# A hybrid encoder block on one core: projection pairs issued in traced order, merges and residual by accumulating transfers

## The chip, the core and the metric

The kernel runs on one core of a Trainium2 chip. The core has five engines, each with its own instruction queue: TensorE (PE in the profile, with its weight loads shown as PEld), VectorE (DVE), ScalarE (ACT), GpSimd (POOL) and SyncE (SP). Sixteen DMA engines move data between device memory and the on-chip memory; a transfer is asked for on the queue of SP, ACT or POOL. The metric is the device time of one execution in microseconds, the median of several runs.

## What is computed

One layer of an encoder on 1024 tokens of 1024 channels: a mixer with two branches, then an MLP. Cut from the reference:

```python
h = rmsnorm(x, g_pre_mix)
proj = jnp.einsum('bsd,de->bse', h, w_in)            # u_pool 512 wide | q | k | v, 8 heads of 64
y_pool = jnp.einsum('bsc,cd->bsd', multiscale_pool(u_pool, w_pool_mix, pool_scale), w_br_pool)
o_sb = stick_breaking_attention(q, k, v)
y_sb = jnp.einsum('bsc,cd->bsd', o_sb, w_br_sb)
gates = jax.nn.sigmoid(jnp.einsum('bsd,de->bse', h, w_gate) + b_gate)
merged = gates[..., :D_MODEL] * y_pool + gates[..., D_MODEL:] * y_sb
x = x + rmsnorm(jnp.einsum('bsd,de->bse', merged, w_out), g_post_mix)
h2 = rmsnorm(x, g_pre_mlp)
a = jnp.square(jax.nn.relu(jnp.einsum('bsd,df->bsf', h2, w_up)))
x = x + rmsnorm(jnp.einsum('bsf,fd->bsd', a, w_down), g_post_mlp)
```

Pooling takes, for each of four groups of 128 channels, the trailing mean over 2, 4, 8 or 16 tokens minus the token itself, then a 128 x 128 map. Stick-breaking attention weighs token s for token t by sigmoid(z_ts) times the product of (1 - sigmoid(z_tj)) over the tokens j between them.

## The kernel before

All tensors lie with channels on the 128 partitions and tokens along the free axis, in two halves h of 512 tokens. Every product runs in three passes: each operand is split into a high part (a cast on ACT) and a low part (source minus high part, on DVE), and PE adds high x high, high x low and low x high. One 128 x 128 weight block against 512 tokens is thus three matmuls (`mm3`, lines 96 to 106).

The Tile framework orders the instructions of each engine before the program runs: it takes the traced order as priority, simulates the engines, and lets whatever is ready go first. An edge (`issue_after`, `add_manual_dep`) keeps two instructions in a wanted order. The order that results is fixed; at run time an engine waits at the head of its queue.

The stages, in order of time:

- **Input** (`phase_in`). Norm of x, the u and v projections, and the operands of the pairs: b11, b21, b22 and the sums t1 to t4, each with a high and a low part (`fill_operand`, line 1056). Its end also traces the first pair's weights (lines 454 to 480): a1, the adds of lines 513 to 517, and the splits s0 (sb) and w (sa).
- **Projection pairs** (`phase_project`). Gates, q and k are done two output blocks at a time by Winograd's form of Strassen's scheme: seven products of half size in place of eight. The 12 pairs are listed in `PAIRS` (line 491): gates 0 to 4, then q and k, then gates 5 to 7. Each `product` (line 659) is 12 matmuls into one of seven PSUM banks that are taken in turn. Its order is a1 on b11, a1 on b21, sb on t2, sa on t3, sa on t1, a22 on t4, sb on b22. DVE and ACT evict the banks; `result` (line 527) puts a sigmoid on a gate and stores it to `gscr`, or splits q and k and stores them to `qscr`. The last pair but one begins the first two products of the last.
- **Beside the pairs.** After each product two generators advance one step: `sw_weights` (line 493), which loads and splits the next pair's weights through three raw buffers and four steps, and `later` (line 546), which does the pooling (window sums on DVE, four buffers m0 to m3, a split into ph and pq, two times three matmuls, stores to `yscr`) and then the values (`vpair`, `vs`, stores to `sscr`). In the first 36 products every sixth gives `later` a second step. Every third of the first 48 products lets POOL start one of 40 transfers that sum weights for the MLP in device memory (`weight_sums`, line 1285).
- **Attention** (`phase_attention`, line 947). For each half g and head: scores, sigmoid (ACT), a scan (DVE, line 791), transposes on PE (line 804), a split of them into ahi (ACT) and alo (DVE, line 815), and the product with v (line 830). Jobs fill PE in between, dealt by the list `deal` in line 959: `job_pool`, `job_merge` (line 900, gate times product, plus the pooled branch from `bscr`, then a split into mg) and `job_out`. `fetch` (line 731) loads their gates; tiles named gt have four buffers.
- **After attention** (`phase_post`, `chain`, line 1062). The second half's merges and output, then for each half h: norm, residual, second norm and the operands of the up product, issued in small steps (`yield` with a step number) beside the matmuls. The residual of h = 1 comes through xr tiles that SP loads.
- **MLP** (`phase_mlp`, `down`). First 32 half-products whose results go to `pscr`, then 16 up pairs of five products each. `pair_raw` (line 1152) loads a pair's weights, `pair_b` and `pair_a` add and split them, `quarter` (line 1229) loads two stored products on ACT's queue. Then the down product, with its own loads chained by `load_in` (line 1325), and the last norm.

Names of the profile: sw and dbr and d are PSUM banks, wraw and wrawx raw weights, whi and wlo a split in the common buffers, s0, s1, a0, a1 the splits of sb and a22, h and ht operands of the pairs, T a score tile.

## Time and profile before

| | us |
|---|---|
| median of 3 runs | 1281.68 |
| lowest, highest | 1280.98, 1282.2 |
| profiled execution | 1283.02 |
| its span, first to last instruction | 1281.1 |
| mean granted TensorE clock | 0.997 of full speed |

| transfers by queue | packets | MB | share of 16 engines |
|---|---|---|---|
| SP (q1) | 65696 | 165.28 | 37.2% |
| POOL (q0) | 30992 | 91.13 | 25.4% |
| ACT (q10) | 13536 | 25.57 | 6.1% |

How to read the rows below. A line such as L104 is the line of the kernel that issued the instruction; products all run through lines 102 to 106, so the tile names tell them apart. `[2.59 <-DVE u L699]` behind an instruction means that its engine was idle for 2.59 us before it, until the DVE instruction of line 699 that wrote u had ended. A row of stages gives, for each engine, busy time and instructions. Matmul durations overlap: each is shown from its start to its modelled end, while the next one has already begun. Instructions in a group row are counted behind an x, followed by their busy time and the mean of one in nanoseconds.

### The profile page before, as it was taken

The numbers are of one execution on the slowest core, as the hardware profiler recorded it, in microseconds if no ns is written. First come the engines' busy times: TensorE is split into PE (matmuls) and PEld (weight loads), VectorE is DVE, ScalarE is ACT, GpSimd is POOL, SyncE is SP. The second block draws the span as 40 slices with busy tenths as digits, with TensorE's granted clock in tenths as the row PEclk, the third lists the DMA queues.
The fourth block names the chain that finished last, engine by engine and source line by source line (L and its number), as shares of the span: only waits on it lengthen the run. The fifth ranks groups of instructions, "written<-read, shape, count | busy, mean of one in ns | idle before, by whom it ended". The sixth has DMA issues, their size and how long they took to land.

```text
span 1281.1 us, 16198 instructions
## 1 busy us (share of the span) xinstructions
PE 1247.4 (97%) x5707; PEld 1022.0 (80%) x5707; DVE 970.6 (76%) x1311; ACT 621.9 (49%) x994; POOL 179.3 (14%) x319
## 2 busy tenths in 40 slices
PE   9999989999989999999999999999999999999998
PEld 6887768887877877777778878888888888888887
DVE  8759687776588898777777978888865564776985
ACT  7247344333455556554556635545554443344452
POOL 1212112342101011101101002221221110001000
PEclk9999999999999999999999989999999999999999
DMA  6586878977898774346638756766549997556552
GB/s 217 167 228 173 247 185 252 327 244 240 324 314 315 236 222 137 80 109 220 216 123 286 216 203 224 252 218 242 198 164 318 302 305 241 197 197 246 185 202 67
DMA packets 110306, 283.00 MB, mean 221 GB/s; under 512 B 12465, under 2 KB 17585, under 8 KB 109073
## 3 DMA queue, kind: packets, MB, share of 16 engines
q1 hardware_dynamic: 65696, 165.28, 37.2%
q0 software_dynamic: 30992, 91.13, 25.4%
q10 hardware_dynamic: 13536, 25.57, 6.1%
q8 instruction: 45, 0.74, 0.2%
q14 instruction: 37, 0.29, 0.1%
HBM read 208.52 MB, written 94.37 MB: 236 GB/s over the span
## 4 chain that ended last, share of the span: by engine, by line
PE 59%; DVE 8%; DMA 3%; issue 2%; ACT 2%; ACTq 0%; DVEq 0%; SPq 0%
PE d L104 16%; PE d L106 16%; PE d L105 16%; PE o L830 2%; DVE T L791 2%; PE dbr L106 2%; PE dbr L105 2%; PE dbr L102 2%; PE at L804 2%; DMA wraw<-w 1%; DVE wlo L75 1%; DVE alo L815 1%; DMA gt<-gscr 1%; PE z L787 1%; PE z L784 1%
## 5 line engine op out<-in xcount | busy, mean ns | idle before, releaser
L105 PE MATMUL d<-blo,whi 128*128 128x512 f32 (+1 forms) x456 | 172.3, 378 | 0.0
L106 PE MATMUL d<-bhi,wlo 128*128 128x512 f32 (+1 forms) x456 | 171.9, 378 | 0.0
L104 PE MATMUL d<-bhi,whi 128*128 128x512 f32 (+1 forms) x456 | 168.7, 378 | 0.0
L105 PEld LDWEIGHTS d<-blo,whi 128*128 128x128 f32 x456 | 85.7, 188 | 16.1
L106 PEld LDWEIGHTS d<-bhi,wlo 128*128 128x128 f32 x456 | 85.8, 188 | 15.8
L104 PEld LDWEIGHTS d<-bhi,whi 128*128 128x128 f32 x456 | 85.5, 188 | 16.0
L791 DVE TENSOR_TENSOR_SCAN T<-T,past 128x256 f32<-128x256 f32 (+5 forms) x64 | 84.5, 1347 | 5.8 <-ACT T L789 5.5
L105 PE MATMUL d<-b_lo,whi 128*128 128x512 f32 x196 | 76.3, 390 | 0.5 <-DVE b_lo L1060 0.5
L104 PE MATMUL d<-b_hi,whi 128*128 128x512 f32 x196 | 75.3, 391 | 0.6 <-ACT b_hi L1059 0.6
L106 PE MATMUL d<-b_hi,wlo 128*128 128x512 f32 x196 | 74.8, 390 | 0.0
L75 DVE TENSOR_TENSOR wlo<-wraw,whi 128x1024 fp32r<-128x1024 f32 x45 | 54.9, 1219 | 24.4 <-ACT whi L74 24.4
L74 ACT CAST whi<-wraw 128x1024 fp32r<-128x1024 f32 x45 | 47.4, 1054 | 49.6 <-DMA wraw<-w 17.1
L814 ACT CAST ahi<-at 128x512 fp32r<-128x512 f32 (+1 forms) x96 | 44.6, 483 | 48.5 <-PE at L804 40.2
L815 DVE TENSOR_TENSOR alo<-at,ahi 128x512 fp32r<-128x512 f32 (+1 forms) x96 | 50.7, 549 | 19.8 <-ACT ahi L814 19.5
L1351 DVE TENSOR_TENSOR wlo<-slots_hi,whi 128x1024 fp32r<-128x1024 f32 x29 | 35.5, 1224 | 37.7 <-ACT whi L1349 37.6
L1349 ACT CAST whi<-slots_hi 128x1024 fp32r<-128x1024 f32 x29 | 30.5, 1052 | 68.5 <-PE d L105 62.3
L1349 ACT CAST whi<-slots_lo 128x1024 fp32r<-128x1024 f32 x27 | 28.4, 1054 | 63.4 <-PE d L105 53.1
L104 PE MATMUL sw<-h_hi,whi 128*128 128x512 f32 x144 | 56.5, 393 | 2.0 <-ACT vs L619 0.8
L105 PE MATMUL sw<-h_lo,whi 128*128 128x512 f32 x144 | 56.1, 389 | 0.0
L106 PE MATMUL sw<-h_hi,wlo 128*128 128x512 f32 x144 | 55.5, 390 | 0.1
L104 PE MATMUL d<-t_hi,whi 128*128 128x512 f32 x132 | 52.7, 399 | 2.5 <-ACT whi L1166 2.5
L789 ACT ACTIVATE T<-z 128x256 f32<-128x256 f32 (+3 forms) x96 | 44.3, 500 | 19.9 <-PE z L787 10.9
(443 smaller groups left out, 3425.7 us busy)
## 6 DMA issues: line engine op xcount, KB each, us to landing
wraw<-w SPq DMA_DIRECT2D x57, 512.0 KB, 4.9
ext_b<-ascr SPq DMA_DIRECT2D x40, 512.0 KB, 7.1
wscr<-w POOLq DMA_DIRECT2D x32, 512.0 KB, 8.9
slots_hi<-w SPq DMA_DIRECT2D x10, 1024.0 KB, 7.7
slots_lo<-w SPq DMA_DIRECT2D x10, 1024.0 KB, 8.4
qq<-qscr SPq DMA_DIRECT2D x32, 256.0 KB, 5.9
pscr<-p SPq DMA_DIRECT2D x32, 256.0 KB, 4.5
u<-pscr ACTq DMA_DIRECT2D x32, 256.0 KB, 4.6
```

Source lines behind the costliest of these rows:

```text
L74: nc.scalar.copy(hi, raw)
L75: self.last_lo = nc.vector.tensor_sub(lo, raw, hi.bitcast(F32)).ins
L102: nc.tensor.matmul(ps, wh, rh, start=first and i == 0, stop=False)
L104: nc.tensor.matmul(ps, wh, rh, start=first and i == 0, stop=False)
L105: nc.tensor.matmul(ps, wh, rl, start=False, stop=False)
L106: self.last_mm = nc.tensor.matmul(ps, wl, rh, start=False, stop=last and i == n - 1).ins
L789: self.after = nc.scalar.activation(f, z[:, :n], AF.Sigmoid, scale=-1.0)
L791: nc.vector.tensor_tensor_scan(f[:, ::-1], f[:, ::-1], past[:, ::-1], 1.0, ALU.mult, ALU.max)
L814: nc.scalar.copy(hi[:, c:], at[:, c:])
L815: nc.vector.tensor_sub(lo[:, c:], at[:, c:], hi[:, c:].bitcast(F32))
L1349: last_split[0] = nc.scalar.copy(hi, src).ins
L1351: last_split[1] = nc.vector.tensor_sub(lo, src, hi.bitcast(F32)).ins
```

## The change

- **Order.** `in_order` adds an edge from each instruction to the next one of the same engine, for everything that is traced in the loop over the pairs on PE, DVE, ACT and POOL. SP is left out. The input stage, with the first pair's weights, is traced before the loop.
- **Weights.** A split is now two steps, high part and low part (`split_steps`), and every product gives two steps to the weights, with the step of `later` between them. A pair's loads are asked for in the first step of the pair before; six empty steps (three products) stand ahead of its first split. A generator that has steps left goes on in the next pair. In the input stage each call is doubled.
- **Pooling and values.** `later` gets one step a product. Window buffers alternate, ph and pq are split by halves of 512 tokens through one buffer, each half's three matmuls come one step after its split, the next u is loaded before the mean, and the stores to `yscr` move from POOL to ACT. Values use m2 and m3 alone; the next pair of loads is asked for a step earlier.
- **Pairs.** Gates 0 to 6 come first, then q and k, then gate 7. The low part of q and k overwrites the evicted tile, two high parts share a buffer, and the stores are one per part: six a result for q, four for k, on POOL. Weight sums start with 12 products in place of 16; four more start in the late heads.
- **Attention.** The first two gates are fetched ahead of the y loads. In the first half's merges, DVE's add of the pooled branch is replaced by a transfer on POOL that adds `bscr` into the tile; the split of a merged tile is traced one merge later, on ACT and DVE. The deal of the second half is 16, 16, 14, 12, 12, 12, 13, 13.
- **After attention.** For h = 1 the residual is added by a POOL transfer from x into each of eight tiles; store, square and sum follow three tiles later.
- **MLP.** The loads of stored products stand behind a weight cast on ACT's queue, and the first load of the down stage behind the third up pair's loads.

```diff
+                next(first)
...
-    PAIRS = [("g", i) for i in range(5)] + [("q", 0), ("k", 0), ("q", 1), ("k", 1)] + [("g", i) for i in range(5, 8)]
+    PAIRS = [("g", i) for i in range(7)] + [("q", 0), ("k", 0), ("q", 1), ("k", 1), ("g", 7)]
...
-        w["a1"] = self.split_weights(r1, self.wp, "w", 3)
+        for _ in range(6 * (i > 0)):
+            yield
+        w["a1"] = yield from self.split_steps(r1, self.wp, "w", 3)
         yield
         pool = self.sw_pools[i % 2]
-        w["a22"] = self.split_weights(a22, pool, f"a{i % 2}", 1, 512)
+        w["a22"] = yield from self.split_steps(a22, pool, f"a{i % 2}", 1, 512)
         nc.vector.tensor_add(a22, a21, a22)
+        yield
...
-        w["sb"] = self.split_weights(r1, pool, f"s{i % 2}", 1)
+        w["sb"] = yield from self.split_steps(r1, pool, f"s{i % 2}", 1)
         yield
-        w["sa"] = self.split_weights(r2, self.wp, "w", 3)
+        w["sa"] = yield from self.split_steps(r2, self.wp, "w", 3)
...
+        if not self.stage:
+            e = self.staged([P, 2, H], F32R, f"{kind}s")
+            self.stage = [e[:, 0, :], e[:, 1, :]]
+        hi = self.stage.pop(0)
+        nc.scalar.activation(hi, t, AF.Copy, scale=sc)
...
-            out=e[:, 1, :], in0=t, scalar=sc, in1=e[:, 0, :].bitcast(F32), op0=ALU.mult, op1=ALU.subtract
...
+        parts = (hi.bitcast(F32), t, hi.bitcast(F32)) if kind == "q" else (hi.bitcast(F32), t)
...
+            scr = self.qscr[kind == "k"][2 * f + b]
+            for n, e in enumerate(parts):
+                nc.gpsimd.dma_start(scr[64 * n : 64 * n + 64, c], e[64 * b : 64 * b + 64])
...
-                n = 1 + i % 2
+                if late is not None:
+                    nc.scalar.dma_start(self.yscr[1][:, g - 1, :], late)
+                    late = None
                 nxt = whole(n, name="win")
...
+            if g < 3:
+                nxt_u = u_load(g + 1)
...
-            ph, pq = whole(3 - n, F32R, "ph"), whole(3 - iu, F32R, "pq")
-            nc.scalar.copy(ph, cur)
-            nc.vector.tensor_sub(pq, cur, ph.bitcast(F32))
+            d = None
+            for h in range(3):
+                c = slice(h * H, h * H + H)
+                if d is not None:
+                    a = slice(h * H - H, h * H)
+                    nc.scalar.activation(cur[:, a].bitcast(F32R), d, AF.Copy, scale=sc)
...
+                pp = self.mx.tile([P, 2, H], F32R, name="pp", tag=f"m{n}")
+                ph, pq = pp[:, 0, :], pp[:, 1, :]
+                nc.scalar.copy(ph, cur[:, c])
+                nc.vector.tensor_sub(pq, cur[:, c], ph.bitcast(F32))
+                yield
+                d = newbank() if h else self.zps.tile([P, H], F32, name="dm", tag="o", bufs=1)
+                self.mm3(d, [(wmh[:, g, :], wml[:, g, :], ph, pq)])
+                yield
+            nc.scalar.dma_start(self.yscr[0][:, g, :], cur)
+            late = u
+            yield
...
+            if t < NK - 1:
+                p = v_load(t + 1)
+            nc.scalar.copy(hi.bitcast(F32R), lo)
+            nc.vector.tensor_sub(lo.bitcast(F32R), lo, hi)
+            yield
+            nc.gpsimd.dma_start(self.sscr[t], v.rearrange("p h x -> p (h x)"))
             yield
...
+    def in_order(self):
+
...
+        last, prev = traced[-1], {}
+        yield
+        while True:
+            traced = self.nc.cur_bb.bb.instructions
+            start = next(k for k in reversed(range(len(traced))) if traced[k] is last) + 1
+            for i in traced[start:]:
+                if i.engine.name not in engines:
+                    continue
+                if i.engine in prev:
+                    self.tc.add_manual_dep(i, prev[i.engine], info, reason="in order")
+                prev[i.engine] = i.name
+            last = traced[-1]
...
-            next(nxt, None)
+            for gen in nxt:
+                next(gen, None)
             next(bg, None)
+            for gen in nxt:
+                next(gen, None)
             c = next(count)
-            if c % 6 == 5 and c < 36:
-                next(bg, None)
-            if c % 3 == 2 and c < 48:
+            if c % 3 == 2 and c < 36:
...
+        order = self.in_order()
         for i, (kind, f1) in enumerate(self.PAIRS):
+            next(order)
...
+            nxt[:-1] = []
+            if i + 1 < len(self.PAIRS):
+                nxt.append(self.sw_weights(i + 1))
...
+        next(order)
...
+        with tc.issue_after(self.head_load):
+            self.fetch(1)
...
+                self.fetches[key] = self.staged_in(self.gscr[8 + e][:, c])
...
                 if g or h > 3:
-                    self.sum_pieces(zero, 1)
+                    self.sum_pieces(zero, 1 + (g and h > 3))
...
+        if h:
+            nc.vector.tensor_add(t, t, q)
+        else:
+            nc.gpsimd.dma_start(t, self.bscr[e][h], accum_op=ALU.add)
...
+        self.merged.append((e, h, t))
+        if h or e == 7:
+            self.merge_split()
+            self.merge_split()
+        elif e:
+            with self.tc.issue_after(self.after.ins):
+                self.merge_split()
+
+    def merge_split(self):
+        nc = self.nc
+        if self.merged:
+            e, h, t = self.merged.pop(0)
+            hi, lo = self.mg[h]
+            nc.scalar.copy(hi[:, e, :], t)
+            nc.vector.tensor_sub(lo[:, e, :], t, hi[:, e, :].bitcast(F32))
...
-        deal = [[5] * 4 + [4] * 4, [18, 18, 16, 11, 11, 11, 11, 12]]
+        deal = [[5] * 4 + [4] * 4, [16, 16, 14, 12, 12, 12, 13, 13]]
...
+        lag = 3 * h
+        for n in range(8 + lag):
+            if n < 8:
+                yield 6 - early + 3 * n
+                m = mix[n]
+
+                with self.tc.issue_after(self.last_lo):
+                    nc.vector.scalar_tensor_tensor(
+                        out=m, in0=m, scalar=self.gn[:, V_POST_MIX + n : V_POST_MIX + n + 1], in1=r,
+                        op0=ALU.mult, op1=ALU.mult,
+                    )
+                    if h == 0:
+                        nc.vector.tensor_add(m, m, xr[n])
+                if h:
+                    nc.gpsimd.dma_start(m, self.x[h][:, n, :], accum_op=ALU.add)
+            e = n - lag
...
+    def split_weights(self, *where):
...
+    def split_steps(self, src, pool, tag, bufs, room=1024):
         nc = self.nc
         n = src.shape[-1]
         hi = pool.tile([P, room], F32R, name=f"{tag}hi", tag=f"{tag}hi", bufs=bufs)[:, :n]
         lo = pool.tile([P, room], F32R, name=f"{tag}lo", tag=f"{tag}lo", bufs=bufs)[:, :n]
         self.last_hi = nc.scalar.copy(hi, src).ins
+        yield
         self.last_split = nc.vector.tensor_sub(lo, src, hi.bitcast(F32)).ins
         return hi, lo
...
-        ps = quarter(0)
+        with tc.issue_after(first):
+            ps = quarter(0)
...
+            behind = self.last_hi
...
+            with tc.issue_after(behind):
+                ps = quarter(i + 1)
...
-        loaded = [None]
+        loaded = [self.third]
```

More of the change, by code (lines that the diff above doesn't have):

```diff
@@ L217, in build @@
         self.op7, self.sw, self.heads = {}, {}, {}
+        self.stage = []
         self.phase_in()
@@ new lines, in later, with v_load @@
+            nc.scalar.dma_start(self.yscr[0][:, g, :], cur)
+            late = u
+            yield
+        nc.scalar.dma_start(self.yscr[1][:, 3, :], late)
+        def v_load(t):
+            p = self.mx.tile([P, 2, H], F32, name="vpair", tag="m2")
+            for j in range(2):
+                nc.scalar.dma_start(p[:, j, :], self.vscr[t * P + j : t * P + j + P, :])
+            return p
+        yield
+        yield
+        p = v_load(0)
+        yield
+        yield
+        yield
+        for t in range(NK):
+            v = self.mx.tile([P, 8, P], F32, name="vs", tag="m3")
+            hi, lo = v[:, :, 0:64], v[:, :, 64:128]
+            a, b = (p[:, j, :].rearrange("p (h x) -> p h x", h=8) for j in range(2))
+            nc.vector.tensor_sub(lo, a, b)
+            yield
+            if t < NK - 1:
+                p = v_load(t + 1)
+            nc.scalar.copy(hi.bitcast(F32R), lo)
+            nc.vector.tensor_sub(lo.bitcast(F32R), lo, hi)
+            yield
+            nc.gpsimd.dma_start(self.sscr[t], v.rearrange("p h x -> p (h x)"))
@@ L590, in later @@
             yield
             yield
-            ds = [self.zps.tile([P, H], F32, name="dm", tag="o", bufs=1), newbank()]
-            for h, d in enumerate(ds):
-                c = slice(h * H, h * H + H)
-                self.mm3(d, [(wmh[:, g, :], wml[:, g, :], ph[:, c], pq[:, c])])
-                nc.scalar.activation(cur[:, c].bitcast(F32R), d, AF.Copy, scale=sc)
-                nc.vector.scalar_tensor_tensor(
-                    out=u[:, c].bitcast(F32R), in0=d, scalar=sc, in1=cur[:, c], op0=ALU.mult, op1=ALU.subtract
-                )
@@ L634, in sum_piece_with @@
         self.tc.add_manual_dep(next(self.wsums).ins, ins.name, info, reason="weight sums")
+    def in_order(self):
+        traced, engines = self.nc.cur_bb.bb.instructions, ("PE", "DVE", "Activation", "Pool")
+        info = mybir.DependencyInfo(mybir.DependencyClass.NoSync, mybir.DependencyReason.DATA)
+        last, prev = traced[-1], {}
+        yield
+        while True:
[8 more added lines that the diff above has]
+            last = traced[-1]
+            yield
     def run(self, gen):
@@ L948, in phase_attention @@
         tc, nc = self.tc, self.nc
-        self.oo, self.mg, self.outs = {}, {}, {}
+        self.oo, self.mg, self.outs, self.merged = {}, {}, {}, []
         self.bank = lambda: self.dps.tile([P, H], F32, name="dbr", tag="d")
@@ L1080, in chain @@
         acc2 = ch.tile([P, H], F32, name="acc2", bufs=1)
-        for e in range(8):
-            yield 6 - early + 3 * e
-            m = mix[e]
-            with self.tc.issue_after(self.last_lo):
-                nc.vector.scalar_tensor_tensor(
-                    out=m, in0=m, scalar=self.gn[:, V_POST_MIX + e : V_POST_MIX + e + 1], in1=r,
-                    op0=ALU.mult, op1=ALU.mult,
-                )
-                nc.vector.tensor_add(m, m, xr[e])
+        lag = 3 * h
[4 more added lines that the diff above has]
+                with self.tc.issue_after(self.last_lo):
+                    nc.vector.scalar_tensor_tensor(
+                        out=m, in0=m, scalar=self.gn[:, V_POST_MIX + n : V_POST_MIX + n + 1], in1=r,
+                        op0=ALU.mult, op1=ALU.mult,
+                    )
+                    if h == 0:
[3 more added lines that the diff above has]
+            e = n - lag
+            if e < 0:
+                continue
+            m = mix[e]
             nc.gpsimd.dma_start(self.xscr[h][e], m)
@@ L1156, in pair_raw @@
             t = big[:, j, :] if i % 2 else self.wp.tile([P, 1024], F32, name="wraw", tag="wraw", bufs=2)
-            self.nc.sync.dma_start(t, self.w[O_UP + f])
+            ins = self.nc.sync.dma_start(t, self.w[O_UP + f]).ins
+            if i == 2:
+                self.third = ins
             raw += [t[:, :512], t[:, 512:]]
         return raw
-    def split_weights(self, src, pool, tag, bufs, room=1024):
+    def split_weights(self, *where):
+        steps = self.split_steps(*where)
+        while True:
+            try:
+                next(steps)
+            except StopIteration as done:
+                return done.value
+    def split_steps(self, src, pool, tag, bufs, room=1024):
         nc = self.nc
@@ L1219, in phase_mlp @@
                 nxt = {"sb": self.pair_b(raw, sums[0], self.wp, "w", 3)}
+                first = self.last_hi
         nxt["a22"] = self.split_weights(raw[3], self.wp, "w", 3)
```

60 lines of the change are left out of this document (12 added, 48 removed).

## The prediction

> **What bounds the kernel now.** I read the busy totals first, then the busy time by stage, the waits of PE, and the timeline at each stall.
>
> ```profile
> PE 1247.4 (97%) x5707; PEld 1022.0 (80%) x5707; DVE 970.6 (76%) x1311; ACT 621.9 (49%) x994; POOL 179.3 (14%) x319
> ```
>
> PE is the bound, and the change removes no matmul. What can be won is PE's idle time, 1281.1 - 1247.4 = 33.7 us, and what a stall costs around it. Busy time by stage (the columns are window, length, then PE, PEld, DVE, ACT and POOL busy, granted clock, DMA share, GB/s); the stages are projection pairs, first and second attention half (the second in two parts), and ten us at the start of the up pairs:
>
> ```profile
> 98.20:345.70 247.50, 238.26 (x1033) 192.33 (x1033) 187.93 (x273) 103.89 (x143) 61.21 (x98) 1.00 0.81 247
> 345.70:440.00 94.30, 89.02 (x467) 73.95 (x466) 76.78 (x111) 51.08 (x125) 10.11 (x32) 1.00 0.85 297
> 440.00:503.00 63.00, 58.71 (x310) 48.51 (x310) 58.55 (x71) 37.12 (x79) 6.86 (x14) 1.00 0.71 210
> 503.00:578.00 75.00, 71.30 (x376) 57.98 (x374) 55.33 (x65) 46.51 (x97) 8.15 (x18) 1.00 0.38 92
> ...
> 738.00:748.00 10.00, 7.45 (x19) 5.11 (x18) 5.30 (x7) 2.99 (x4) 0.00 (x0) 0.66 0.94 333
> ```
>
> PE idles 9.2 us in the pairs, 5.3, 4.3 and 3.7 us in attention, 2.6 us at 738. These 25.1 us are what the edits can reach; the rest lies at the two ends of the kernel and around 620 and 650. Who is waited for (engine, waiting line, releaser, total us, times, longest):
>
> ```profile
> PE o L830 <- DVE alo L815: 6.2, 10, 1.6
> PE at L804 <- DVE alo L815: 4.6, 4, 1.5
> PE sw L104 <- DVE u L699: 2.6, 1, 2.6
> PE sw L104 <- ACT whi L1166: 2.6, 2, 1.5
> PE d L104 <- ACT whi L1166: 2.5, 1, 2.5
> ```
>
> Attention waits for VectorE, the pairs for late evictions and late weight splits, the up pairs once for a split.
>
> A stall costs more than its idle time. At the longest one of the pairs:
>
> ```profile
> 297.74 0.39 PE L105 MATMUL sw<-h_lo,whi 128*128 128x512 f32 x1
> 297.96 0.39 PE L106 MATMUL sw<-h_hi,wlo 128*128 128x512 f32 x1
> 300.94 0.50 PE L104 MATMUL sw<-ht_hi,a1hi 128*128 128x512 f32 x1 [2.59 <-DVE u L699]
> 301.27 0.40 PE L105 MATMUL sw<-ht_lo,a1hi 128*128 128x512 f32 x1
> ```
>
> Undisturbed starts are 0.227 us apart (the first two rows, rounded; the stage's row gives (247.5 - 11.9) / 1033 = 0.228, with the loss found next). From 297.96 to 301.27 there are 3.31 us where 0.45 would do: 2.86 lost for 2.59 idle. I add 0.27 us to each of the ten stalls of the pairs: **11.9 us lost there**. At 738 there is a larger surcharge. Ten us at 0.227 hold 44 matmuls, the row shows 19 at a mean clock of 0.66: 25 missing, 5.7 us lost with 2.55 idle. So about 3.1 us are slow clock after the stall. The equally long stall at 300.9 was not followed by one:
>
> ```profile
> 300.00:302.00 2.00, 1.06 (x5) 0.88 (x6) 1.97 (x4) 0.59 (x1) 1.16 (x2) 1.00 0.50 105
> ```
>
> The price of a restart after 2.5 us idle is thus 0 or 3.1 us. The Trainium skill (TensorE: Matmul & The Clock Gate, What's actually happening) has the array fall to half clock after an idle window of about 3.4 us. By that rule neither stall should have been slowed, and at 738 the trace disagrees; a stall of 5 us would be slowed by it, one below 3 us would not.
>
> **Projection pairs: what goes.** With weights asked three products ahead (3 x 12 x 0.227 = 8.2 us) a split no longer waits for its load:
>
> ```profile
> wscr<-w POOLq DMA_DIRECT2D x32, 512.0 KB, 8.9
> slots_hi<-w SPq DMA_DIRECT2D x10, 1024.0 KB, 7.7
> ...
> sscr<-vs POOLq DMA_DIRECT2D x8, 512.0 KB, 6.8
> ...
> slots_hi<-w POOLq DMA_DIRECT2D x4, 1024.0 KB, 15.7
> ...
> yscr<-win POOLq DMA_DIRECT2D x4, 512.0 KB, 8.4
> ```
>
> A plain megabyte lands in 7.7 us (issue to landing, last column), two 512 KB weights come to about that. In traced order each low half stands two or more products (5.4 us) ahead of its matmul, and a bank is taken again six products later at the earliest. VectorE's work fits: 187.9 of 247.5 us, and only 1.0 product's worth of pooling now goes with each product. What stays: in order, VectorE stands still for stores. A window buffer is taken again two products (5.4 us) after its store to yscr, which lands in 8.4 us; a value tile two products after its store to sscr (6.8). That is 3 us three times and 1.4 us seven times, under the 5.4 us of cover, so PE should see little. POOL gets 32 more q/k stores and loses eight yscr ones, which ACT issues; four of 16 weight-sum pieces move to attention. POOL was busy 61 of 247 us, so this hides there. I let 15% of the stalls stay: **-10.1** (ends: -11.9, and 0 if the in-order waits replace the old ones).
>
> **Projection pairs: what comes.** The fixed order forbids something that PE does now. In the first pair the third product is sb on t2; its split is late (VectorE, then ACT, then PE):
>
> ```profile
> 105.50 0.70 DVE L517 TENSOR_TENSOR wraw<-wraw 128x512 f32<-128x512 f32 x1
> 106.10 4.31 DVE L1060 TENSOR_TENSOR h_lo<-x,h_hi 128x512 fp32r<-128x512 f32 x7
> ...
> 112.12 1.23 DVE L1167 TENSOR_TENSOR s0lo<-wraw,s0hi 128x1024 fp32r<-128x1024 f32 x1
> ```
>
> ```profile
> 108.17 1.05 ACT L1166 CAST s0hi<-wraw 128x1024 fp32r<-128x1024 f32 x1
> ```
>
> ```profile
> 103.69 0.39 PE L104 MATMUL sw<-ht_hi,whi 128*128 128x512 f32 x1
> ...
> 109.33 0.43 PE L104 MATMUL sw<-ht_hi,s0hi 128*128 128x512 f32 x1
> ...
> 113.41 0.50 PE L106 MATMUL sw<-ht_hi,s0lo 128*128 128x512 f32 x1
> ```
>
> PE has done both a1 products at 103.7. It now takes sa, then a22, and comes back to sb when s0lo ends at 113.35: no idle time. Chained, it must begin sb at 103.7, idles to 109.3, does two matmuls, and idles to 113.4: 113.41 - 103.69 - 0.45 = **+9.3 us**. Nothing in the diff hastens this split: the sums and splits of pair 0 are traced in the input stage, outside the chain, and the doubled step calls there only undo the added pauses. The low end: s0hi straight after L517 (106.2 + 1.05) and s0lo after that (1.23) end at 108.5, +4.4. One idle stretch is 5.4 us, longer than the 2.5 that brought a slow clock at 738, so I add that row's **+3.1** (low end 0). The pairs as a whole: -10.1 + 9.3 + 3.1 = **+2.3**, between -7.5 and +12.4 with the ends above.
>
> **Attention.** Two rows show why the second half is short of VectorE:
>
> ```profile
> ACT mg_hi L924 <- DVE gt L918: 20.4, 9, 5.7
> ```
>
> ```profile
> L918 DVE TENSOR_TENSOR gt<-gt 128x512 f32<-128x512 f32 x12 | 8.2, 686 | 0.1
> ```
>
> VectorE is busy 58.55 of 63 us in 440 to 503, where all eight first-half merges lie (18 + 18 + 16 steps: 20 of pooling, 32 of merges). Eight adds of 0.69 go, 5.5 us; six of the 52 steps go to the later heads (16 + 16 + 14). ACT, which must make ahi for PE's next product, now stands 20.4 us for the merged tile; a split put one merge later does not wait for VectorE any more. It waits for an accumulating transfer instead, with the scores' scans and the ahi copies queued behind it on ACT. The trace has no 256 KB one into SBUF. Ends, from the rows of transfers above: a quarter of the 1 MB one, 3.9 us, and the 512 KB one, 8.9 us. A merge takes 52 steps in 63 us, four steps 4.9 us, so at the low end nobody waits. I take 5 us (256 KB is nearer to half of 8.9, with its fixed part), which is hidden. (The Trainium skill, DMA: Bandwidth & Descriptors, Anatomy of one DMA, puts a GpSimd transfer at 2.0 us plus its bytes at 436 GB/s. By that estimate 1 MB takes 4.4 us and 256 KB 2.6 us, and rival 2 below would be out; the trace's 15.7 us for 1 MB disagrees.) Of the 4.3 us idle in this part I let 3.5 go. The first half starts on gates that were fetched behind the y loads and now go ahead: 1.5 of 5.3. The later heads get more filler but also more splits: 0. **-5**, between -8 (all idle time of the second half) and, at 8.9 us, +12 (rivals).
>
> **Up pairs.** The second raw of pair 0 is asked for when the last low half frees its buffer, and VectorE is late with that:
>
> ```profile
> 729.65 1.22 DVE L75 TENSOR_TENSOR wlo<-wraw,whi 128x1024 fp32r<-128x1024 f32 x1
> 730.79 3.09 DVE L1060 TENSOR_TENSOR t_lo<-mix,t_hi 128x512 fp32r<-128x512 f32 x5
> 736.54 0.69 DVE L1175 TENSOR_TENSOR sums<-wraw 128x512 f32<-128x512 f32 x1 [2.67 <-DMA wraw<-w]
> ```
>
> Then come the load, sums and split: the 5.7 us lost at 738. Holding the product loads behind the first split leaves the load alone on the queues, and eight adds (5.5 us at 0.69) leave VectorE before this. Against that, each row of x now comes by an accumulating transfer with three steps of lag; the last must land before the channel sum. I take **-3.5** (ends -5.7, and +8: eight transfers at 8.9 us with three in flight take 24 us, where 8 x 3 steps of three matmuls give 16). The order of slots behind the third pair changes no stall: after 748 PE doesn't idle until the end.
>
> **Sum** for the profiled execution (1283.0 us, 1.9 more than its span): +2.3 - 5 - 3.5 = -6.2. The median of the runs shown, 1281.7, lies 1.3 lower: 1281.7 - 6.2 = **1275.5**.
>
> **Rivals.**
> 1. *The first pair does not stall much.* PE's third product starts soon after its split if the new order of the planner moves s0lo ahead of the seven h_lo. For: nothing needs these seven before the fifth product. Against: they stand ahead now. Then the pairs give -10.1 + 4.4 without slow clock, -5.7 where the forecast has +2.3: **1267**; without any stall 1263.
> 2. *Accumulating transfers are late* (slower). Place: the split of a merged tile on ACT. At 8.9 us each of seven merges holds ACT 8.9 - 4.9 = 4 us, 28 us, of which ACT's idle share (26 of 63 us) covers 11; attention then is -5 + 17 = +12, and the chain after it loses its 3.5: 1275.5 + 17 + 3.5 = 1296, at 7 us, by the same working and half of the 3.5, about **1286**. It decides from about 6.4 us, where it eats the 6.2. For: a megabyte into SBUF took twice its plain time. Against: the merges lie where DMA is busy only 0.71.
> 3. *The change doesn't make the pairs or attention better.* The in-order waits for stores take the place of the old stalls (0 for -10.1), with VectorE faster in attention and the up pairs: 2.3 + 10.1 - 5 - 3.5 = +3.9, with the small first stall of rival 1 -4.1; between them **1282**. For: DMA is busy 0.81 in the pairs, so a landing can exceed the 10.9 us (four products) from which PE would feel it. Against: no wait of the pairs now names a store as PE's releaser.
>
> **Chances.** Forecast 0.45, rival 1 0.24, rival 2 0.13, rival 3 0.18. The range leaves out the far ends of 1 and 2: 1263 to 1286. Faster by over 0.2% (below 1279.1; 0.2%, or 2.6 us, is about what a measurement of this kernel tells from no change): 0.38 of the forecast, all of rival 1 and 0.05 of rival 3, 0.67. Slower (above 1284.2): 0.11 of rival 2, 0.05 of the others, 0.16. Same: 0.17.
>
> **What would show it.** Right: PE stands at 103.7 for s0hi and s0lo of the first pair, with a granted clock below 1 behind it, and hardly idles in the other eleven; ACT's wait for mg_hi falls below 10 us; the stall at 738 is below 1.5 us. Wrong: no idle time in the first pair (rival 1); ACT waiting for the accumulating transfers, with ahi and PE behind it (2); VectorE waiting for yscr and sscr stores, with PE behind it (3).

## The result: 3.5% slower, and the profile after

The changed kernel takes **1326.73 us** (1326.3 to 1328.63), the kernel before 1281.94 us beside it: a ratio of 1.0353 [1.0335, 1.0371]. The forecast was 1275.5 us, with a range that ended at 1286.

The busy totals of the page, changed kernel:

```profile
PE 1266.1 (96%) x5707; PEld 1032.3 (78%) x5707; DVE 967.5 (73%) x1299; ACT 624.6 (47%) x998; POOL 202.4 (15%) x359
```

The same 5707 matmuls keep TensorE busy 18.7 us longer (1247.4 before), and its idle time in the span grows from 33.7 to 1324.6 - 1266.1 = 58.5 us. The mean granted clock fell from 0.997 to 0.981 of full speed, which over 1324.6 us is about that much time. Busy time by stage of the changed kernel, with the columns of the prediction (window, length, PE, PEld, DVE, ACT, POOL, granted clock, DMA share, GB/s): the first 30 us of the pairs, the other pairs, attention in three parts, the stage after it, the first halves of the up products:

```profile
98.00:128.40 30.40, 22.62 (x85) 17.65 (x84) 25.41 (x40) 15.38 (x24) 7.45 (x10) 0.83 0.63 166
128.40:375.60 247.20, 228.72 (x951) 182.08 (x950) 165.35 (x233) 88.23 (x121) 60.24 (x106) 0.97 0.72 215
375.60:476.00 100.40, 89.54 (x450) 74.09 (x449) 75.76 (x109) 51.29 (x126) 10.14 (x32) 0.95 0.80 279
476.00:541.00 65.00, 59.46 (x302) 48.37 (x301) 56.14 (x65) 35.01 (x75) 12.21 (x22) 0.97 0.74 208
541.00:619.40 78.40, 76.01 (x402) 62.49 (x401) 57.66 (x68) 49.54 (x102) 11.25 (x22) 1.00 0.47 115
619.40:688.80 69.40, 68.30 (x294) 54.82 (x295) 54.00 (x78) 33.27 (x54) 8.44 (x14) 1.00 0.61 197
688.80:784.00 95.20, 90.37 (x389) 71.97 (x388) 71.15 (x101) 56.17 (x90) 11.49 (x16) 1.00 0.68 212
```

By the starts of TensorE's first product in each stage, the pairs took 277.6 us (247.5 before), attention 243.8 (232.4), the first halves of the up products 95.3 (93.2), everything else the same within 0.3 us. That is +30.1, +11.4 and +2.1 of the span's +43.5. Attention's part lies wholly ahead of its first merge product: from the first scores to there it took 100.7 us (87.9 before), from there on 143.1 (144.6 before).

What the pairs lose can be counted: each matmul takes 0.227 us, and the rest is lost. The first 30 us hold 85 matmuls, 19.3 us: **11.1 lost** (the kernel before loses 0.7 there). The other pairs hold 951, 215.9 us: **31.3 lost**, where before lost 11.8. The prediction had +12.4 for the first pair and -10.1 for the rest. The first came true, +10.4, and in the very place; the timeline of TensorE, changed kernel:

```profile
108.54 0.80 PE L104 MATMUL sw<-ht_hi,s0hi 128*128 128x512 f32 x1 [4.92 <-ACT s0hi L1248]
...
112.62 0.80 PE L106 MATMUL sw<-ht_hi,s0lo 128*128 128x512 f32 x1 [2.85 <-DVE s0lo L1250]
```

The rest did not go; it grew by 19.5 us. Who waits for whom in the other pairs shows what is new. ACT's waits from 128 to 375, changed kernel (waiting line, releaser, total us, times, longest):

```profile
ACT c L537 <- DVE c L738: 28.4, 5, 8.6
ACT v L537 <- DVE v L743: 18.3, 6, 3.7
ACT u L537 <- DVE u L745: 14.6, 7, 2.6
ACT c L537 <- DVE c L720: 12.7, 7, 2.6
```

VectorE's:

```profile
DVE wlo L1250 <- ACT whi L1248: 14.1, 10, 2.3
DVE vs L639 <- DMA sscr<-vs: 13.6, 4, 5.7
DVE u L605 <- ACT win L604: 11.6, 6, 2.8
DVE s1lo L1250 <- ACT s1hi L1248: 6.6, 4, 2.2
```

and the largest of TensorE's, which stand for casts (s1hi, pp) and subtractions (wlo):

```profile
PE sw L104 <- ACT s1hi L1248: 4.1, 2, 2.9
PE sw L104 <- ACT pp L612: 4.0, 2, 2.3
PE dm L104 <- ACT pp L612: 2.9, 1, 2.9
PE sw L106 <- DVE wlo L1250: 2.8, 5, 0.8
```

ACT stands 74 us at the sigmoid (L537) for VectorE's additions, and VectorE stands for ACT's casts. One turn of it, VectorE's timeline in the second pair (start, duration, what, idle time before it):

```profile
129.04 0.68 DVE L743 TENSOR_TENSOR v<-v,sw 128x512 f32<-128x512 f32 x1
131.96 1.23 DVE L1250 TENSOR_TENSOR s1lo<-wrawx,s1hi 128x1024 fp32r<-128x1024 f32 x1 [2.24 <-ACT s1hi L1248]
133.10 0.68 DVE L745 TENSOR_TENSOR u<-u,sw 128x512 f32<-128x512 f32 x1
136.60 0.75 DVE L605 SCALAR_TENSOR_TENSOR u<-dm,vt,win 128x512 fp32r<-128x512 f32 x1 [2.82 <-ACT win L604]
137.27 0.68 DVE L613 TENSOR_TENSOR pp<-win,pp 128x512 fp32r<-128x512 f32 x1
```

ACT's, and then TensorE's:

```profile
129.75 0.72 ACT L537 ACTIVATE v<-v,vt 128x512 f32<-128x512 f32 x1 [3.41 <-DVE v L743]
130.51 0.33 ACTq L538 DMA_DIRECT2D gscr<-v  x1
130.88 1.05 ACT L1248 CAST s1hi<-wrawx 128x1024 fp32r<-128x1024 f32 x1 [0.40 <-ACT v L537]
133.82 0.72 ACT L537 ACTIVATE u<-u,vt 128x512 f32<-128x512 f32 x1 [1.89 <-DVE u L745]
134.57 0.33 ACTq L538 DMA_DIRECT2D gscr<-u  x1
134.94 1.04 ACT L1248 CAST whi<-wraw 128x1024 fp32r<-128x1024 f32 x1 [0.40 <-PE sw L106]
...
136.47 0.61 ACT L612 CAST pp<-win 128x512 fp32r<-128x512 f32 x1
```

```profile
137.13 0.50 PE L104 MATMUL sw<-pp,wm 128*128 128x512 f32 x1 [2.34 <-ACT pp L612]
```

Follow it by the clock: VectorE adds v (129.04), only then ACT takes the sigmoid of v (129.75), only then ACT casts s1hi (130.88), only then VectorE subtracts s1lo (131.96), only then VectorE adds u (133.10), only then ACT takes the sigmoid of u (133.82). VectorE's and ACT's queues are wound into one chain, which makes one turn a product here: 0.68 for the addition, 0.72 + 0.40 for the sigmoid and the issue behind it, 1.05 for the cast, 1.23 for the subtraction, **4.1 us where a product takes 2.72**. The product of v had ended at 125.95 and that of u at 128.67; both additions waited in line. A pair has four such splits and four results in its seven products, so not every turn has all five links: over the about 77 products of the other pairs the loss is 0.4 us a product, not 1.4. In the end the pooling's cast is late and TensorE stands. (The Trainium skill, PSUM — Partial Sum Buffer, Engine vs sequencer instructions, says that the queues of ScalarE, VectorE and GpSimdE are strictly first in, first out; this trace agrees: the addition of u, whose product had ended at 128.67, stands behind the subtraction of s1lo until 133.10.) I call this the **ring**.

### The profile page after: what moved, and what is told of

It is laid out like the page before. It is cut to its first block, busy times and chain, and to the rows that moved or that the text cites. A ratio compares the mean times of both kernels' runs of the same rounds, so it can differ in the third digit from the quotient of the medians.

```text
span 1324.6 us, 16154 instructions
## 1 busy us (share of the span) xinstructions
PE 1266.1 (96%) x5707; PEld 1032.3 (78%) x5707; DVE 967.5 (73%) x1299; ACT 624.6 (47%) x998; POOL 202.4 (15%) x359
## 4 chain that ended last, share of the span: by engine, by line
PE 67%; issue 12%; DVE 10%; DMA 5%; ACT 3%; POOL 2%; ACTq 0%; SPq 0%; POOLq 0%; DVEq 0%
PE d L104 15%; PE d L106 15%; PE d L105 15%; PE o L878 2%; PE dbr L105 2%; PE dbr L106 2%; PE dbr L102 2%; PE at L852 2%; DVE T L839 1%; PE sw L106 1%; POOL qscr L552 1%; PE sw L104 1%; PE sw L105 1%; DMA mix<-x 1%; DVE wlo L75 1%
## 5 line engine op out<-in xcount | busy, mean ns | idle before, releaser
L839 DVE TENSOR_TENSOR_SCAN T<-T,past 128x256 f32<-128x256 f32 (+6 forms) x64 | 84.6, 1346 | 10.6 <-ACT T L837 10.4
L75 DVE TENSOR_TENSOR wlo<-wraw,whi 128x1024 fp32r<-128x1024 f32 x45 | 54.8, 1217 | 23.7 <-ACT whi L74 22.4
L837 ACT ACTIVATE T<-z 128x256 f32<-128x256 f32 (+3 forms) x96 | 44.4, 498 | 30.6 <-PE z L835 22.0
L852 PE MATMUL at<-eye,T 128*128 128x128 f32 x288 | 48.6, 281 | 10.3 <-DVE alo L863 5.6
```

Of the source, the lines that this page charges most:

```text
L75: self.last_lo = nc.vector.tensor_sub(lo, raw, hi.bitcast(F32)).ins
L837: self.after = nc.scalar.activation(f, z[:, :n], AF.Sigmoid, scale=-1.0)
L839: nc.vector.tensor_tensor_scan(f[:, ::-1], f[:, ::-1], past[:, ::-1], 1.0, ALU.mult, ALU.max)
L852: t = nc.tensor.transpose(at[:, r * P : r * P + P], a[r][:, s * P : s * P + P], self.eye)
```

## The experiments

Sixteen kernels, in the order in which they ran; "before" ran beside each group, on the same chip, at medians of 1278.8 to 1281.6 us. The ratio goes by the kernel before that ran beside. Stage lengths (pairs, attention, first halves of the up products) are from the one profile of each kernel.

| kernel | median us | ratio to before, 95% | pairs | attention | up |
|---|---|---|---|---|---|
| before | 1281.9 | 1 | 247.5 | 232.4 | 93.2 |
| after | 1326.7 | 1.0353 [1.0335, 1.0371] | 277.6 | 243.8 | 95.3 |
| e1 no order | 1294.7 | 1.0109 [1.0088, 1.0129] | 251.5 | 238.7 | 95.5 |
| e2 order on TensorE only | 1301.2 | 1.0166 [1.0145, 1.0186] | 246.0 | 251.5 | 96.6 |
| e3 order from pair 1 | 1315.4 | 1.0274 [1.0236, 1.0312] | 265.4 | 247.7 | 95.1 |
| e5 late results | 1300.5 | 1.0160 [1.0137, 1.0182] | 250.7 | 245.3 | 96.4 |
| e6 before + merges | 1278.9 | 1.0000 [0.9985, 1.0015] | 248.0 | 234.9 | 88.6 |
| e7 before + up stage | 1288.9 | 1.0073 [1.0049, 1.0098] | 249.7 | 233.3 | 93.2 |
| e8 late results, from pair 1 | 1290.6 | 1.0086 [1.0062, 1.0111] | 242.2 | 243.6 | 97.2 |
| e9 no order, heads exchanged | 1291.6 | 1.0099 [1.0073, 1.0125] | 251.9 | 233.7 | 96.0 |
| e10 order on all but TensorE | 1330.8 | 1.0391 [1.0372, 1.0410] | 280.0 | 246.4 | 95.3 |
| e11 e9 with q/k earlier | 1295.7 | 1.0116 [1.0095, 1.0137] | 242.2 | 246.6 | 96.8 |
| e12 e1 with faster pooling | 1302.8 | 1.0187 [1.0138, 1.0235] | 253.4 | 243.4 | 96.3 |
| e13 before + early weights | 1280.1 | 0.9998 [0.9976, 1.0020] | 248.2 | 233.3 | 92.2 |
| e14 e11, second head elsewhere | 1294.8 | 1.0101 [1.0057, 1.0146] | 244.9 | 245.3 | 98.2 |
| e15 e8, rest as before | 1282.4 | 1.0018 [0.9998, 1.0038] | 243.1 | 241.4 | 91.5 |
| e16 e15, heads early | 1279.4 | 0.9988 [0.9968, 1.0008] | 245.8 | 236.6 | 88.6 |
| e17 e16, last pair free | 1279.2 | 0.9986 [0.9968, 1.0005] | 245.3 | 236.5 | 88.6 |

The pairs end where attention's first scores begin, so a late start of attention is counted in "pairs" (e1, e9, e12). Behind the first merge product attention takes 142.7 to 146.1 us in all eighteen profiles (before 144.6): what differs between them lies ahead of it.

### Which order costs

**e1**, the order taken out:

```diff
-        order = self.in_order()
         for i, (kind, f1) in enumerate(self.PAIRS):
-            next(order)
...
         self.run(bg)
-        next(order)
```

> The changed kernel without the fixed order: the four engines are left to the planner, the traced steps stay. Theory A (in a fixed order VectorE's late add, ScalarE's sigmoid, its next cast and VectorE's next subtraction form one ring that is longer than a product's 2.72 us): the pairs' loss of 43.6 us goes back to about the 13.5 us of before, 30 us less, and the kernel to about 1297 us (attention and up pairs keep their +13.5). Rival B (the new trace itself, its asks and stores, is late): the pairs stay within 10 us, the kernel above 1316.

1294.7. Its products run as the prediction wanted them, all 1033 matmuls in the first row; the second row is TensorE waiting behind them (same columns):

```profile
98.90:335.95 237.05, 235.83 (x1033) 193.16 (x1031) 188.63 (x277) 103.34 (x146) 68.65 (x118) 1.00 0.78 228
335.95:350.40 14.45, 0.00 (x0) 0.02 (x1) 1.78 (x3) 2.06 (x3) 0.00 (x0) 0.62 0.95 331
```

2.6 us are lost in 237.1, no stall is over 0.6 us, and the products take 10.4 us less than in the kernel before (237.1 against 247.5). So the order cost the pairs 40 us of products, and what kept this kernel at +1.1% lies behind them (below).

**e2** and **e10** divide the order between the engines:

```diff
-        traced, engines = self.nc.cur_bb.bb.instructions, ("PE", "DVE", "Activation", "Pool")
+        traced, engines = self.nc.cur_bb.bb.instructions, ("PE",)                             # e2
+        traced, engines = self.nc.cur_bb.bb.instructions, ("DVE", "Activation", "Pool")       # e10
```

> The changed kernel with the fixed order kept on TensorE alone; VectorE, ScalarE and GpSimd are free. Theory A: the ring between VectorE and ScalarE is gone, pair 0's stall of 11 us stays, pairs about 258 us (277.6 - 19), kernel about 1307. Rival C (TensorE's own order is the cost, because it can't go ahead with another product): no change, 1322 to 1330. Rival B: no change either.

> The changed kernel with the fixed order kept on VectorE, ScalarE and GpSimd, TensorE free. Theory A (the ring lies between VectorE and ScalarE, whatever TensorE does): only the first pair's stall goes, about 1315 us, and TensorE's waits in the later pairs stay on casts and subtractions. Rival D (only the orders together stall, a free TensorE works around late splits): near the 1294.7 us without any order.

With TensorE alone in order, the first pair still stands and nothing else does. (e2 ended 6 us below its forecast of 1307, and by other parts than forecast: its pairs took 246.0 us, not 258, and its attention 19 us more than before's, 17.5 of them ahead of the first merge product. Why was not tried.) TensorE's waits from 98 to 345, e2:

```profile
PE sw L104 <- ACT s0hi L1248: 5.1, 1, 5.1
PE sw L106 <- DVE s0lo L1250: 2.9, 1, 2.9
PE sw L105 <- DVE pp L613: 0.7, 1, 0.7
```

With the other three in order and TensorE free, the first pair's loss halves (5.2 us lost in the first 30.6) and the other pairs stand more than in the changed kernel, 40.3 us lost in 249.4, always for a split. TensorE's waits from 128 to 377, e10:

```profile
PE sw L104 <- ACT s1hi L1248: 11.3, 4, 4.1
PE sw L104 <- ACT s0hi L1248: 8.3, 3, 4.2
PE sw L106 <- DVE wlo L1250: 3.3, 1, 3.3
```

At 1330.8 it missed its forecast of 1315 on the high side, and refutes the rival that a free TensorE works around late splits: the ring is VectorE's and ACT's own. (GpSimd was in order too; it was not tried apart.)

**e3** starts the order at the second pair; **e5** leaves it on all four engines and cuts the ring at one link, by tracing each finished block's sigmoid (or q/k split) and its store one product later, behind that product's casts; **e8** does both:

```diff
+        order = None                                     # e3, e8
         for i, (kind, f1) in enumerate(self.PAIRS):
-            next(order)
+            if i == 1:
+                order = self.in_order()
+            if i:
+                next(order)
```

```diff
+        kept = []                                        # e5, e8
+        def give(*args):
+            if kept:
+                self.result(*kept.pop())
+            if args:
+                kept.append(args)
         def product(w, at, name):
...
             for gen in nxt:
                 next(gen, None)
+            give()
...
-            self.result(kind, f, 0, c11, 1.0)
+            give(kind, f, 0, c11, 1.0)
```

> The changed kernel with the fixed order starting at the second pair. By the prediction's step for the first pair: 11 us less (7.8 us idle and 3.3 us of slow clock between 98 and 128 us), kernel about 1316. If the first pair's stall is only put off to the next products: within 3 us of 1326.7.

> The changed kernel, all four engines in order, but each finished block's sigmoid or q/k split and its store is traced one product later, behind that product's weight cast and pooling steps. Theory A: ScalarE makes its casts while the product runs, the ring is cut, pairs 1 to 11 lose 15 to 25 us less, kernel 1302 to 1312; pair 0's stall stays. Rival B or C: within 4 us of 1326.7.

> The kernel of the late results, with the fixed order starting at the second pair too. The two costs lie in different places, so they add: 1300.5 - 11 = about 1289.5 us. If one hides the other (the stall of the first pair only moves): above 1296.

All three came close to their forecasts: 1315.4, 1300.5 (1.5 us below its range), 1290.6. The windows of e5 show that one link is enough; the first pair's stall stays, and the other pairs lose 5.0 us (947 matmuls) where the changed kernel loses 31.3:

```profile
99.30:130.00 30.70, 22.47 (x88) 17.62 (x88) 26.92 (x43) 16.96 (x27) 7.45 (x10) 0.83 0.62 166
130.00:350.00 220.00, 217.06 (x947) 178.05 (x946) 164.46 (x233) 88.21 (x121) 61.27 (x108) 0.99 0.79 238
```

The numbers of instructions are the same: only ACT's casts stand ahead of the sigmoid that waits. Up to 340 us ACT no longer stands for the addition of v and 1.4 us for that of u (18.3 and 14.6 in the changed kernel's pairs), and VectorE stands 0.3 us for whi instead of 14.1.

### The merges and the up stage alone

**e6** is the kernel before with the eight accumulating transfers, the later splits of the merged tiles and the new shares of filler; **e7** is the kernel before with the change's up stage.

> The kernel before with the change's merges alone: eight accumulating transfers instead of VectorE's adds, each split one merge later, and the new shares of filler. Theory: the stalls for alo near the merges are the merges' own (a transfer of about 4.5 us with ScalarE standing in order behind it), attention 4 to 7 us longer than before's 232.4 us, kernel 1286 to 1289. Rival: the merges pay as forecast (-5 us, kernel about 1277), and attention's loss in the changed kernel comes from the late end of the pairs.

> The kernel before with the change's up stage alone: rows of x by accumulating transfers with three steps of lag, quarter loads behind the first split, the third pair's load ahead of later slots. If the +2.1 us seen in the changed kernel is its own: kernel about 1284. If it depends on what goes ahead: the forecast -3.5 us, about 1278.

e6: no difference (1.0000 [0.9985, 1.0015]), so neither -5 nor the theory's +4 to +7. The transfer was sized well (the page's row of the changed kernel, KB each and median us from issue to landing):

```profile
gt<-bscr POOLq DMA_DIRECT2D x8, 256.0 KB, 4.5
```

but ACT still stands for the merged tile, now for the transfer instead of VectorE: 12.6 us in 375 to 541 of the changed kernel, 12.9 in 345 to 503 before, 16.8 in e6.

```profile
ACT mg_hi L987 <- DMA gt<-bscr: 12.6, 7, 4.3
```

Taking VectorE's 5.5 us of adds away did not shorten that stage. e6's attention is 2.5 us longer in its profile, all of it ahead of the first merge product (90.6 against 87.9); the 4.6 us by which its up stage is shorter, with the same up code as before, show how much the first split there varies: in the six profiles with that code its stall is 0 to 2.51 us.

e7: slower by 0.7%, and its profile holds a part of it only (pairs +2.2, the stage after attention +2.5, span +5.5); where the rest lies is not known. The stall at the up pairs' first split is 3.51 us, not shorter than before's 2.51. The six profiles with the up code of before have 88.6 to 93.2 us in the first halves, the twelve with the change's 93.2 to 98.2. The stage shows where the time goes. The load of the second raw is asked for when the last low half (L75) has freed its buffer; SP's rows, changed kernel:

```profile
765.02 0.37 SPq L70 DMA_DIRECT2D wraw<-w  x1
...
774.07 0.37 SPq L1229 DMA_DIRECT2D wraw<-w  x1
```

That is 76.2 and 85.2 us into the stage; before's rows at 721.01 and 730.89 are 73.3 and 83.2 us into it. It is a chain of load, cast, subtraction, next load, and its last links came 2.0 to 2.9 us later, although eight additions had left VectorE. VectorE's queue is a part of that chain: from 755 to 778 it has no idle time, and its last low half starts at 772.29, 1.7 us after the cast for it ended. What in the change's up stage makes the chain later was not tried.

### What is late when the pairs are repaired

e1 left 14.5 us in one wait, at the very start of attention (timeline of TensorE, e1):

```profile
350.41 0.77 PE L829 MATMUL z<-kk,qq 128*128 128x512 f32 x1 [14.46 <-DMA kk<-qscr]
```

Head 0's keys go into the buffer of the value tiles, whose last store was issued at 334.91, at the end of the products. In the kernel before, that last store was issued at 322.48, 23 us ahead of the end, and head 0's keys were asked for earlier still. SP's timeline, before:

```profile
289.68 0.33 SPq L762 DMA_DIRECT2D kk<-qscr  x1
```

Four runs tried to free this start, and a fifth gave the kernel before the change's weights: **e9** exchanges the buffers of the first two heads (`tag=f"m{2 * h}"` for `m{2 - 2 * h}`, and the same for the keys), **e11** moves the q/k pairs one pair earlier as well, **e14** gives the second head a buffer of attention's own pool, **e12** lets pooling and value tiles take a second step every sixth product, as before did, **e13** puts the change's schedule of weights into the kernel before.

> The kernel without the fixed order, with the first two heads' queries and keys loaded into each other's buffers (head 0 takes those of the q/k results instead of those of the value tiles). In the kernel without the fixed order TensorE ended the pairs at 335.6 us and stood 14.5 us for head 0's keys. If the buffers of the value tiles held these loads: 8 to 14 us less than 1294.7, about 1283. If the queue of stores and loads holds them in any buffer: above 1291.

> The kernel without the fixed order and with exchanged buffers for the first heads, and with the q/k pairs one pair earlier (two gate pairs behind them), so that head 0's keys and the y loads queued behind them do not wait for the last q/k stores. If the queue's order holds attention back: scores start about 340 us instead of 350, kernel 1279 to 1285. If the transfers themselves are the wall (queues 1.03 busy at 400 GB/s from 330 us on): scores start later than 347, kernel above 1289.

> The kernel without the fixed order, with a second step of pooling and value tiles every sixth product up to the 36th, as before: the value tiles end six products (16 us) earlier. If one step a product is what puts their last store (334.9 us) and so head 0's keys behind the last product: scores start about 338 us instead of 350, kernel 1280 to 1285. If the loads themselves or the outputs of the last pairs hold attention: above 1290.

> The kernel before with the change's schedule of the weights alone: asked three products ahead, splits in two steps, two steps a product; the pooling, the pair order and the planner's freedom are those of before. If the late splits are what the pairs lose: 3 to 8 us less than before, about 1275. If attention cannot start before its loads have landed, whatever the pairs win: within 2 us of before.

> The kernel of the early heads, with the second head's queries and keys loaded into buffers of attention's own pool instead of those of the value tiles. If the value tiles' buffers hold attention: the 8.3 us stall for its keys and its slow clock go, kernel 1283 to 1287. If the loads come late whatever the buffer (the queue behind the y loads, 400 GB/s): above 1292.

None of the five reached the number of its first theory. Three of the four without the order freed a load and found another late: in e9 SP stood 40.6 us, in two waits, for k stores before it could ask for keys, in e11 scores began at 341.4 but the second head's keys were 8.3 us late, in e14 they were still 2.8 us late behind a first scan that was 4.1 us late, and in e12 the value tiles ended no sooner (last store 339.85) and the products 13 us later than in e1. Full queues alone do not explain it: between 338 and 360 us e1, e9 and e11 have them busy 0.88 to 1.03 at 317 to 378 GB/s, and the kernel before 1.04 at 404 GB/s with hardly a stall; there the first loads were asked for sooner. e13 does not settle what asking for weights earlier is worth: its loads go out when before's do (113.77 and 129.71 us, against 113.38 and 129.32), because SP stands for the subtraction that frees a raw buffer (52.6 us for s0lo, 53.3 before), and the waits for whi at 148 and 172 us stand there as before. Which of e1's other differences (pooling in small steps, the order of the pairs, the stores) takes them away was not tried.

Then the repaired pairs of e8 were put with before's attention, merges and up stage (**e15**), with the heads' buffers free early (**e16**), and with the last pair out of the order (**e17**):

> The kernel of the late results and the order from the second pair, with attention, merges and the up stage put back to those of before; the pairs alone are the changed ones. If the loss behind them is attention's start (loads, value tiles and heads at the pairs' end): still 1285 to 1290. If it is the changed attention and up code: at or below before, 1274 to 1281.

> The repaired pairs with attention and up stage of before, the q/k pairs one pair earlier and the first two heads' buffers exchanged: head 0 takes those of the q/k results, free a pair earlier, head 1 those of the value tiles, whose last store lay 23 us ahead of the pairs' end. If late first loads are what attention's first part pays: 88 to 91 us instead of 96.9, kernel 1273 to 1278, below before. If not: within 3 us of 1282.

> The same, with the last pair of projections out of the fixed order. If the last additions, held behind the first heads' scans (a stall of 2.45 us for v), are what is left: 2 to 5 us below the kernel of both heads. If the order of the last pair does not matter: within 2 us of it.

e15 is level with before (1.0018): the change's attention and up code cost 8.2 us here, by the profiles 5.7 of it in the up stage. Its pairs are 4.4 us shorter and its attention 9 us longer, all of that up to the first merge product (96.9 us against 87.9). SP, which issues the loads in order, stands for the value tiles' buffer, and the y loads stand behind it. SP's waits from 270 to 350, e15:

```profile
SPq L821 <- DMA sscr<-vs: 11.7, 1, 11.7
```

In e16 this wait is gone, keys are asked for at 312.50 instead of 322.70, and that first part takes 92.1 us; 2.7 of the 4.8 us are paid again in the pairs. The medians of e15 and e16 differ by 3.0 us, but their intervals overlap, and the up stage, whose code is the same, is 2.9 us shorter in e16's profile: what the buffers are worth is not shown. e17 changes nothing more. At 0.9988 [0.9968, 1.0008] e16 can't be told from the kernel before, and none of these beats it by more than the runs can tell.

## Why the prediction was wrong, by its own steps

- **The first pair, +9.3 and +3.1: right.** The stall has 7.8 us idle and 3.3 lost beside it at a granted clock of 0.83, 11.1 us where before loses 0.7; e3 took 11.3 us off the kernel, e8 9.8 off e5. Rival 1 is out.
- **"With weights asked three products ahead a split no longer waits for its load", -10.1: this is the step that failed**, by 29.6 us (+19.5). Word for word it came true: no cast of a pair's weights waits for its load in the other pairs of the changed kernel, where ACT had stood 25 us for them before. But the split still came late: it stood in ACT's queue behind a sigmoid that waited for VectorE. And the waits for loads had not been the price: in e1 ACT stands 29 us for them, and the pairs lose 2.6. The two stalls for whi before, 2.6 of the 9.2 us idle, were not released by a load either. ACT's timeline, before:

```profile
145.47 0.72 ACT L532 ACTIVATE c<-c,vt 128x512 f32<-128x512 f32 x1 [2.48 <-DVE c L692]
...
146.67 1.04 ACT L1166 CAST whi<-wrawx 128x1024 fp32r<-128x1024 f32 x1 [0.47 <-DVE wrawx L515]
```

The cast waited for VectorE's sum of the weights, behind a sigmoid that had waited for VectorE, and TensorE stood 1.49 us. I had added up whether VectorE's work fits (187.9 of 247.5 us), but a fixed order on two engines asks something else: how long is the path that goes back and forth between them in one product. The durations for that sum were in the trace of before, 4.1 us against 2.72.
- **Rival 3 had a part of it.** The waits for stores that it named are there: VectorE stands 13.6 us for sscr and 2.1 for yscr, and one of these waits lies ahead of the stall of 2.93 us at 317.40 (VectorE's timeline, changed kernel):

```profile
304.75 0.69 DVE L639 TENSOR_TENSOR vs<-vpair 128x512 f32<-128x512 f32 x1 [5.66 <-DMA sscr<-vs]
```

  But e5 keeps these waits (13.3 us for sscr) and loses 5.0 us, so by themselves they cost TensorE little; the ring passed them on. Nor did the new stalls equal the old ones, as rival 3 had it: 31.3 us are lost where 11.8 were.
- **And -10.1 would not have been kept**: e1, without the order, has the old stalls gone, its products take 10.4 us less, and attention starts late. The prediction asked what is late next only for TensorE's products; it left out the loads at the seam, which before's order had put 23 us ahead.
- **Attention, -5: wrong, +11.4.** The transfer's landing was right (5 taken, 4.5 measured), and rival 2 with its 6.4 us is out. But ACT's wait changed its releaser and not its size, and e6 is worth nothing either way. The +11.4 are not the merges': 12.8 us more lie ahead of the first merge product and 1.4 less behind it, and e15 still has +9 with before's own attention code. Loads that land late behind the pairs are part of it, as e15's and e16's waits show; the rest stays open.
- **Up pairs, -3.5: wrong, about +2 to +6.** The stall at the first split did not fall below 1.5 us, it rose to 3.26. The step took VectorE's additions for the limit; the trace has a chain of loads, casts and subtractions, and it came later without them. Why it came later stays open.
- **Sum.** From the changed kernel down, by medians: late results -26.2, the first pair out of the order -9.8, before's attention and up code -8.2: from 1326.7 to 1282.4, the time of the kernel before. The kernels before that ran beside these had medians of 1278.8 to 1281.9, so each term is good to about 2 us.

## What to carry to other kernels

Before an order is fixed on several engines, add up the path that goes back and forth between them within one step of the loop; each engine may have idle time, and the loop can still run at the length of that path. In such an order, put what is ready ahead of what waits: an eviction's second half belongs behind the next step's casts. And when a stage is made shorter, look at what must have landed at its end before counting the gain.

## What the runs showed of the hardware

The price of a short stall is not fixed. Four microseconds from the restart, changed kernel, after stalls of 2.85 and 3.26 us (the clock is the third figure from the end):

```profile
159.50:163.50 4.00, 3.98 (x9) 2.89 (x10) 2.42 (x3) 1.14 (x2) 0.95 (x1) 0.50 0.21 70
...
784.10:788.10 4.00, 3.90 (x8) 2.66 (x9) 3.96 (x5) 1.48 (x3) 0.00 (x0) 0.50 1.01 398
```

and e1, behind 2.98 us:

```profile
484.50:488.50 4.00, 4.00 (x22) 3.32 (x23) 3.97 (x5) 2.39 (x6) 0.00 (x0) 1.00 0.99 369
```

Eight or nine matmuls where 17 fit in the one case, full clock in the other (where short transposes are among the 22). Of twelve stalls of 1.7 to 3.3 us in the kernels before, after, e1 and e7, nine were followed by a mean clock of 0.50 to 0.77 over four microseconds, three (2.40, 2.59 and 2.98 us) by 1.00. The Trainium skill names an idle window of about 3.4 us for the fall to half clock (TensorE: Matmul & The Clock Gate, What's actually happening); here shorter stalls were followed by it too. Over the other pairs of the changed kernel the clock is a part of the difference between 18.5 us idle and 31.3 us lost.
